# Last output projection of a two-layer trunk: the order of one product, when its weight sums are added, and how many planner steps the side work takes

## The chip, the cores and the metric

The kernel runs on one core of a Trainium2 chip. The metric is the device time of one execution in microseconds (us). The engines are named as in the profile: PE does the matrix products (PEld its weight loads), DVE, ACT and POOL are the vector, scalar and GpSimd engines, SP only issues DMAs. POOL issues DMAs as well, and all the accumulating ones.

## What is computed

Two layers over 256 tokens of width 2048. Each layer normalizes x, projects it, runs four branches (sparse attention, retention, a gated recurrence, cross-attention), gates and sums them, and adds an output projection:

```
merged = sum over n of sigmoid(gate_n) * (branch_n @ w_branch[n])
x = x + merged @ w_out
```

The change lies in the last of these, `merged @ w_out` of layer 1 and what comes after it: a product of 256 x 2048 by 2048 x 2048, added to x and stored.

## The kernel before

**Number format.** Each float32 factor is split into a rounded high part and a remainder (`whi`, `wlo` for weights; `...h`, `...l` for the other side), and three fast products replace one: high by high, low weight by high, high weight by low. Making the parts of a tile costs one ACT copy (`cut_piece`, line 433) and one DVE subtraction that waits for it (line 435).

**Units.** Weights come in slabs of 512 x 512, each used in two half slabs. A half slab of an ordinary slab (both token halves) is 12 matmuls, a half slab of a "product" (one token half) is 6. There are four buffers of weight parts: parts are cut four half slabs ahead of their use, and the ACT copy of a cut waits until PE has finished the half slab four before.

**The last stage.** The four output columns are numbered 0 to 3. Columns 0 and 1 are done plainly, in slabs (column, row block), for the merged blocks `mg0`, `mg3`, `mg2`, `mg1` in that order. Columns 2 and 3 together are done with one product in eight saved (a Strassen-Winograd scheme): seven products 0 to 6, whose left sides are sums of quarters of the merged matrix, called forms (product 1 uses form `s3`, 3 uses `s1`, 4 uses `s2`, 0 uses `r4`; 2, 5 and 6 use plain quarters), and whose right sides are weights or sums of weight blocks. The sums are built in memory by accumulating DMAs: chain `sumy` passes through products 2, 3, 4 and 6 (the next block is added behind each cut, `LAST_NEXT`), chain `sumx` serves product 1 alone: four base loads on SP, four accumulating DMAs on POOL. Products 0 and 5 use raw weights.

`LAST_ORDER` (line 160) is the order, written by hand: slabs as pairs, products as numbers. In this document half slabs of the stage are counted from 0. Before: (0,0) is 0 and 1, (1,0) 2 and 3, (0,1) 4 and 5, product 2 is 6 to 9, (1,1) 10 and 11, (0,2) 12 and 13, product 1 is 14 to 17, product 3 is 18 to 21, (1,2) 22 and 23, (0,3) 24 and 25, product 4 is 26 to 29, product 0 is 30 to 33, (1,3) 34 and 35, product 5 is 36 to 39, product 6 is 40 to 43. A number in `LAST_BEGIN` says how many half slabs ahead of its product's first one a DMA stage is issued, counted in cuts. Before, the `sumx` base loads come in front of cut 14 - 30 = -16, its adds in front of cut -6; the first `sumy` loads in front of cut -4.

**Side work and the planner.** Everything that isn't a slab is a task, a generator that is resumed between half slabs: `advance` (line 501) calls `Stream.pump` (210) and then cuts the next half slab. `pump` allows two steps behind a slab's half slab and one behind a product's, and none while the planner's account of DVE or ACT stands over `LATE` = 2500 ns behind its account of PE; a task is resumed only when PE's account has passed the end of its last step by `MARGIN` = 500 ns. The account's costs are in lines 111 to 142: a DVE operation of n elements per partition 155 + 1.05 n ns (1230 for 1024, 693 for 512), an ACT copy 215 + 0.8 n (1034 for 1024), a half slab 2720 on PE, one of a product 1360. When a product needs a form that isn't there, its task is forced on (`stream.until`, line 1591). The planner only fixes the order of the instructions in each engine's queue; the engines then run as their waits allow.

**The tasks of the stage.** `merged(d)` (1433) turns a merged block round: a DVE transpose (`mgpi`), 16 small DMAs (`mgp`), a rest of three or four ticks, then `split` (`mg...h` on ACT, `mg...l` on DVE). For block 1, the last, all 16 DMAs go through POOL; the others alternate between POOL and SP. `last_forms` (1442) makes the forms; each is two DVE operations over 512 (`total`, 1270, one planner step each) and two parts (`parts`, 1276, one step each). `second_column` (1556) recombines column 3 behind product 0: `qs - us`, then `us = qs + ...`, then a POOL DMA that adds the residual onto `us`, then `xc - qs`; `us` is stored by SP five ticks later. Product 6 needs `xc - qs` and forces the task on (1594). Behind products 5 and 6, `first_column` (1579) adds on DVE and stores a token half of column 2; the one behind product 6 is the end of the kernel's work.

```
ps, t = {0: (0, 1), 1: (0, 1), 2: (0, 0), 3: (1, 0), 4: (1, 1), 5: (0, 0), 6: (1, 0)}[i]
...
if i == 6 and "less" not in got:
    stream.until(got["second"], lambda: "less" in got)
```

Of the kernel before, what the change touches and what calls it, by code (L numbers as in the profile page):

```python
# [154 lines left out]
DUO, AHEAD, FIRST, MERGED = (2, 0, 3, 1), 10, 0, (0, 3, 2, 1)  # L155
# [1 line left out]
STAGES = ((False, 1, 1), (True, 0, 1), (False, 0, 0), (True, 0, 1), (True, 1, 1))  # L157
LAST_SUM, RING, EARLY = (True, 1, 0), 5, 8
BETWEEN_PRODUCTS = (4, 3, 4, 4, 3, 2, 3)
LAST_ORDER = ((0, 0), (1, 0), (0, 1), 2, (1, 1), (0, 2), 1, 3, (1, 2), (0, 3), 4, 0, (1, 3), 5, 6)  # L160
LAST_RAW, LAST_NEXT = {0: (1, 1), 5: (1, 0)}, {2: (True, 0, 1), 3: (True, 1, 1), 4: (True, 1, 0)}
LAST_BEGIN = {2: ((AHEAD, "y", (False, 0, 0)),), 1: ((3 * AHEAD, "x", (False, 0, 1)), (2 * AHEAD, "x", (True, 1, 1)))}
MOVES, STEPS, BANKS, WARM = 5, 2, 2, 7
MARGIN, LATE = 500.0, 2500.0

# [123 lines left out]
def gemm_plan(wmem, win, wbr, wout):  # L289
# [22 lines left out]
    def last_product(l, i, part):  # L312
# [3 lines left out]
        if not part:  # L316
            for ahead, chain, stage in LAST_BEGIN.get(i, ()):
                begins[len(cuts) - ahead] = chain, stage
# [5 lines left out]
    for l in range(L):  # L324
# [18 lines left out]
        if l + 1 < L:  # L343
# [3 lines left out]
            continue  # L347
        for at in LAST_ORDER:
            if isinstance(at, tuple):
# [14 lines left out]
def trunk(ctx: ExitStack, tc: tile.TileContext, x, xt, memt, ng, qkg, hg, lbl, win, wmem, wbr, wout,  # L364
# [16 lines left out]
    def G(shape, name, dt=F32):  # L381
        return gen.tile(shape, dt, tag="g", name=name)
# [169 lines left out]
    def blocks(u):  # L552
        return u.rearrange("p h (b c) -> p h b c", c=32)
# [670 lines left out]
    for l in range(L):  # L1224
# [45 lines left out]
        def total(out, sign, first, second):  # L1270
            for p in range(2):
                at, a, b = (u[p] if isinstance(u, tuple) else blocks(u[:, 4 * p:4 * p + 4, :]) for u in (out, first, second))
                (ve.tensor_add if sign > 0 else ve.tensor_sub)(at, a, b)
                yield

        def parts(name, out):
            hi, lo = (spool.tile([128, 8, 128], F32R, tag="s", name=name + e) for e in "hl")
            ac.copy(hi, out)
            yield
            ve.tensor_sub(lo, out, hi.bitcast(F32))  # L1280
            yield
            return hi, lo
# [25 lines left out]
        def sigmoid(gt, t, src):  # L1308
            ac.activation(gt[:, t, :], src, AF.Sigmoid, scale=rs[:, t:t + 1])
# [35 lines left out]
        def both(us):  # L1345
            for t in range(2):
                sigmoid(us, t, us[:, t, :])
                yield
            return us
# [92 lines left out]
        def last_forms():  # L1442
            def quarter(b, t):
                return tuple(last_rows[b + p][:, :, 4 * t:4 * t + 4] for p in range(2))

            while not (0 in last_rows and 1 in last_rows):
                yield BLOCKED
            r4 = G([128, 8, 128], "r4")
            yield from total(r4, -1, quarter(0, 0), quarter(0, 1))
            last_made["s3"] = yield from parts("s3", r4)  # L1450
            while len(last_rows) < 4:
                yield BLOCKED
            s1, s2 = (G([128, 8, 128], name) for name in ("s1", "s2"))
            yield from total(s1, -1, quarter(0, 1), quarter(2, 1))
            last_made["s1"] = yield from parts("s1", s1)
            yield from total(s2, -1, s1, quarter(0, 0))
            last_made["s2"] = yield from parts("s2", s2)
            yield from total(r4, 1, s2, quarter(2, 0))
            last_made["r4"] = yield from parts("r4", r4)

        def gated(pg):
# [76 lines left out]
        xh, rs = nx, stream.add(scale_of(nssq, list(nx), 1))  # L1538

    last_ready = stream.add(last_forms())  # L1540
    open_chunks, ends, got = {}, {}, {}

# [13 lines left out]
    def second_column():  # L1556
        qs, us = got["qs"], got["us"]
        ve.tensor_tensor(qs, qs, us[:, 0:1, :].to_broadcast([128, 2, 512]), op=OP.subtract)
        yield
        ve.tensor_tensor(us, qs, us[:, 1:2, :].to_broadcast([128, 2, 512]), op=OP.add)  # L1560
        po.dma_start(us, x1[:, :, 3 * 512:4 * 512], accum_op=OP.add)
        yield
        ve.tensor_sub(got["xc"][:, 1, :], got["xc"][:, 1, :], qs[:, 1, :])
        got["less"] = True
        yield from stream.rest(5)
        sy.dma_start(out[:, :, 3 * 512:4 * 512], us)
# [17 lines left out]
    def last_take(i, part):  # L1584
# [15 lines left out]
        if i == 2:  # L1600
            got["us"] = G([128, 2, 512], "us")
            ac.copy(got["us"][:, 0, :], to)
        elif i == 1:
            got["qs"] = G([128, 2, 512], "qs")
            ac.activation(got["qs"][:, 1, :], to, AF.Copy, scale=-1.0)
        elif i == 3:
            ac.copy(got["us"][:, 1, :], to)
            got["xc"] = residual(2)
        elif i == 4:
            ve.tensor_add(got["us"][:, 0, :], got["us"][:, 0, :], to)  # L1610
        elif i == 0:
            ac.copy(got["qs"][:, 0, :], to)
            got["second"] = stream.add(second_column())
        else:
            first_column(i - 5, to)

    for at in LAST_ORDER:
        if isinstance(at, tuple):
# [61 lines left out]
```

## Time and profile before

| | us |
|---|---|
| median of 3 runs (1820.14 to 1822.33) | 1821.0 |
| the profiled execution | 1821.62 |
| its span in the trace | 1819.9 |
| PE busy | 1799.6 |
| DVE busy | 1369.0 |
| ACT busy | 1077.7 |
| POOL busy | 400.7 |

A trace row gives the start, the duration, the engine, the line, the operation and its tiles (output <- inputs), and in brackets how long the engine had stood idle and what ended that. All helper calls show line 127 (DVE, ACT, POOL) or 145 (PE), so rows are told apart by tiles: `wo` is a plain slab's result, `px` a product's. A PE row's duration is longer than its share, because matmuls overlap: the distance between starts is what counts. "SPq" rows are DMA issues on SP. The DMA list gives, for each kind of issue, the queue, the count, KB of one and the median us from issue to landing.

### The profile page before, as it was taken

What the parts mean: (1) busy time and instruction counts of PE and PEld (TensorE: products, weight loads), DVE (VectorE), ACT (ScalarE), POOL (GpSimd) and SP (SyncE); (2) the same over time, 40 slices, a digit from 0 to 9 for tenths busy, and PEclk for the clock granted to TensorE, in tenths of its full rate; (3) what the DMA queues carried; (4) which work ended last, traced back from release to release, by engine and by line L of the source; (5) the groups of instructions that cost most, each with busy time, mean ns of one, the idle gap of its engine ahead of it and who ended that gap; (6) DMA issues with size and microseconds to landing.
All of it is one profiled execution on the core that took longest, in us unless ns stands there. A gap on an engine that the chain in (4) does not pass through costs nothing.

```text
span 1819.9 us, 24386 instructions
## 1 busy us (share of the span) xinstructions
PE 1799.6 (99%) x8812; PEld 1495.5 (82%) x8812; DVE 1369.0 (75%) x1482; ACT 1077.7 (59%) x1283; POOL 400.7 (22%) x599
## 2 busy tenths in 40 slices
PE   9999999999999999999999999999999999999996
PEld 7889888888888888888888888888888888888875
DVE  5677798786878777677666788887787967767785
ACT  4756565456667656564465656545566755656363
POOL 0022320033332111102123241003322211010420
PEclk9999999999999999999999999999999999999998
DMA  9769965789999899977785995668999989998996
GB/s 330 270 213 288 289 206 187 252 231 268 286 256 285 271 232 273 262 228 243 237 276 173 325 260 180 226 235 243 251 273 279 290 246 240 285 251 274 267 245 182
DMA packets 127401, 459.84 MB, mean 253 GB/s; under 512 B 23472, under 2 KB 44720, under 8 KB 95024
## 3 DMA queue, kind: packets, MB, share of 16 engines
q1 hardware_dynamic: 89200, 356.14, 55.9%
q0 software_dynamic: 37792, 101.88, 28.9%
q8 instruction: 69, 1.13, 0.2%
q14 instruction: 52, 0.43, 0.1%
q10 hardware_dynamic: 288, 0.26, 0.0%
HBM read 428.05 MB, written 6.29 MB: 239 GB/s over the span
## 4 chain that ended last, share of the span: by engine, by line
PE 91%; DMA 4%; DVE 2%; issue 1%; ACT 1%; POOL 0%; SPq 0%; ACTq 0%; DVEq 0%; POOLq 0%
PE u L145 49%; PE px L145 21%; PE bw L145 9%; PE wo L145 5%; PE mv L145 2%; PE mk L145 2%; DMA sumy<-in_wout 1%; DMA mgp<-mgpi 1%; DVE wlo L127 1%; DMA raw<-in_wbr 1%; PE ixrp L145 0%; ACT whi L127 0%; PE mov L145 0%; PE mlg L145 0%; PE bo L145 0%
## 5 line engine op out<-in xcount | busy, mean ns | idle before, releaser
L127 DVE TENSOR_TENSOR wlo<-raw,whi 128x1024 fp32r<-128x1024 f32 (+3 forms) x548 | 644.7, 1186 | 315.7 <-ACT whi L127 309.5
L127 ACT CAST whi<-raw 128x1024 fp32r<-128x1024 f32 (+3 forms) x548 | 559.4, 1024 | 542.9 <-PE u L145 343.3
L127 DVE TENSOR_TENSOR wlo<-sum,whi 128x1024 fp32r<-128x1024 f32 x240 | 288.1, 1220 | 62.6 <-ACT whi L127 55.9
L127 ACT CAST whi<-sum 128x1024 fp32r<-128x1024 f32 x240 | 250.5, 1052 | 99.1 <-PE px L145 51.3
L127 POOL DMA_DIRECT2D sum<-in_win x152 | 137.2, 909 | 608.3 <-DVE wlo L127 560.1
L127 POOL DMA_DIRECT2D mgp<-mgpi x72 | 40.1, 610 | 133.9 <-DVE mgpi L127 67.5
L145 PE MATMUL u<-whi,x01h 128*128 128x512 f32 (+2 forms) x176 | 67.5, 384 | 0.0
L145 PE MATMUL u<-whi,x11h 128*128 128x512 f32 (+2 forms) x176 | 67.5, 384 | 0.0
L145 PE MATMUL u<-whi,x12h 128*128 128x512 f32 (+2 forms) x176 | 67.5, 383 | 0.0
L145 PE MATMUL u<-whi,x02h 128*128 128x512 f32 (+2 forms) x176 | 67.5, 383 | 0.0
L145 PE MATMUL u<-whi,x10h 128*128 128x512 f32 (+2 forms) x176 | 67.4, 383 | 0.0
L145 PE MATMUL u<-whi,x00h 128*128 128x512 f32 (+2 forms) x176 | 67.4, 383 | 0.0
L145 PE MATMUL u<-whi,x13h 128*128 128x512 f32 (+2 forms) x176 | 67.2, 382 | 0.0
L145 PE MATMUL u<-whi,x03h 128*128 128x512 f32 (+2 forms) x176 | 67.2, 382 | 0.0
L145 PE MATMUL u<-wlo,x13h 128*128 128x512 f32 (+2 forms) x176 | 67.1, 381 | 0.0
L145 PE MATMUL u<-wlo,x11h 128*128 128x512 f32 (+2 forms) x176 | 67.1, 381 | 0.0
L145 PE MATMUL u<-wlo,x01h 128*128 128x512 f32 (+2 forms) x176 | 67.1, 381 | 0.0
L145 PE MATMUL u<-wlo,x02h 128*128 128x512 f32 (+2 forms) x176 | 67.1, 381 | 0.0
L145 PE MATMUL u<-wlo,x12h 128*128 128x512 f32 (+2 forms) x176 | 67.1, 381 | 0.0
L145 PE MATMUL u<-wlo,x00h 128*128 128x512 f32 (+2 forms) x176 | 67.1, 381 | 0.0
L145 PE MATMUL u<-wlo,x10h 128*128 128x512 f32 (+2 forms) x176 | 67.1, 381 | 0.0
L145 PE MATMUL u<-whi,x10l 128*128 128x512 f32 (+2 forms) x176 | 67.1, 381 | 0.0
(536 smaller groups left out, 4590.8 us busy)
## 6 DMA issues: line engine op xcount, KB each, us to landing
raw<-in_win SPq DMA_DIRECT2D x180, 1024.0 KB, 6.4
sum<-in_win POOLq DMA_DIRECT2D x152, 512.0 KB, 8.5
sum<-in_win SPq DMA_DIRECT2D x80, 512.0 KB, 6.9
raw<-in_wbr SPq DMA_DIRECT2D x32, 1024.0 KB, 6.6
raw<-in_wout SPq DMA_DIRECT2D x28, 1024.0 KB, 6.7
raw<-in_wmem SPq DMA_DIRECT2D x12, 1024.0 KB, 6.7
sumy<-in_wout POOLq DMA_DIRECT2D x12, 512.0 KB, 10.4
raw<-in_win SPq DMA_DIRECT2D x8, 656.0 KB, 4.2
```

Source lines behind the costliest of these rows:

```text
L127: return call(*args, **kw)
L145: return self.engine.matmul(out, w, x, **kw)
```

## The change

- **Order.** Slab (1,2) moves ahead of products 1 and 3, and these two change places. New half slab numbers: (1,2) is 14 and 15, product 3 is 16 to 19, product 1 is 20 to 23; all others keep theirs. Product 1 is "the single product": it alone uses `sumx`.
- **`sumx`.** Its base loads are issued 34 half slabs ahead of product 1 (in front of cut 20 - 34 = -14), its accumulating DMAs 6 ahead (in front of cut 14).
- **Forms.** Both DVE operations of a form are done in one planner step; since nothing is yielded behind them, the ACT copy of the form's high part falls into the same step. A form takes two steps instead of four.
- **Recombination.** `second_column` does all its DVE operations and the POOL DMA in one step, the first one behind half slab 34 (the first of slab (1,3)).

```diff
-LAST_ORDER = ((0, 0), (1, 0), (0, 1), 2, (1, 1), (0, 2), 1, 3, (1, 2), (0, 3), 4, 0, (1, 3), 5, 6)
+LAST_ORDER = ((0, 0), (1, 0), (0, 1), 2, (1, 1), (0, 2), (1, 2), 3, 1, (0, 3), 4, 0, (1, 3), 5, 6)
...
-LAST_BEGIN = {2: ((AHEAD, "y", (False, 0, 0)),), 1: ((3 * AHEAD, "x", (False, 0, 1)), (2 * AHEAD, "x", (True, 1, 1)))}
+LAST_BEGIN = {2: ((AHEAD, "y", (False, 0, 0)),), 1: ((34, "x", (False, 0, 1)), (6, "x", (True, 1, 1)))}
...
+            def both(*at):
+                for _ in total(*at):
+                    pass
+
             while not (0 in last_rows and 1 in last_rows):
                 yield BLOCKED
             r4 = G([128, 8, 128], "r4")
-            yield from total(r4, -1, quarter(0, 0), quarter(0, 1))
+            both(r4, -1, quarter(0, 0), quarter(0, 1))
...
-            yield from total(s1, -1, quarter(0, 1), quarter(2, 1))
+            both(s1, -1, quarter(0, 1), quarter(2, 1))
             last_made["s1"] = yield from parts("s1", s1)
-            yield from total(s2, -1, s1, quarter(0, 0))
+            both(s2, -1, s1, quarter(0, 0))
             last_made["s2"] = yield from parts("s2", s2)
-            yield from total(r4, 1, s2, quarter(2, 0))
+            both(r4, 1, s2, quarter(2, 0))
...
         ve.tensor_tensor(qs, qs, us[:, 0:1, :].to_broadcast([128, 2, 512]), op=OP.subtract)
-        yield
         ve.tensor_tensor(us, qs, us[:, 1:2, :].to_broadcast([128, 2, 512]), op=OP.add)
         po.dma_start(us, x1[:, :, 3 * 512:4 * 512], accum_op=OP.add)
-        yield
         ve.tensor_sub(got["xc"][:, 1, :], got["xc"][:, 1, :], qs[:, 1, :])
```

## The prediction

> **What bounds the kernel now.** The page first: PE is the bound, and what can be won lies where PE stands still or ends early.
>
> ```profile
> PE 1799.6 (99%) x8812; PEld 1495.5 (82%) x8812; DVE 1369.0 (75%) x1482; ACT 1077.7 (59%) x1283; POOL 400.7 (22%) x599
> ```
>
> Second, one piece of the chain of waits gives the price of a slab, 24 matmuls in 5.44 us; a half slab is 2.72 and one of a product 1.36. Third, PE's rows in order of time through the last stage, which begins at 1718.08:
>
> ```profile
> 1685.61 5.44 PE bw L145 x24
> ```
>
> ```profile
> 1728.74 0.39 PE L145 MATMUL wo<-whi,mg0l 128*128 128x512 f32 x1
> 1730.90 0.50 PE L145 MATMUL wo<-whi,mg3h 128*128 128x512 f32 x1 [1.78 <-ACT mg3h L127]
> ...
> 1732.16 0.50 PE L145 MATMUL wo<-whi,mg3l 128*128 128x512 f32 x1 [0.53 <-DVE mg3l L127]
> ...
> 1737.28 0.39 PE L145 MATMUL px<-whi,mg0h 128*128 128x512 f32 x1
> ...
> 1775.46 0.39 PE L145 MATMUL px<-whi,s2h 128*128 128x512 f32 x1
> ...
> 1780.73 0.39 PE L145 MATMUL px<-whi,s2l 128*128 128x512 f32 x1
> 1783.20 0.50 PE L145 MATMUL px<-whi,r4h 128*128 128x512 f32 x1 [2.08 <-ACT r4h L127]
> ...
> 1786.12 0.80 PE L145 MATMUL px<-whi,r4l 128*128 128x512 f32 x1 [2.19 <-DVE r4l L127]
> ...
> 1787.14 0.63 PE L145 MATMUL px<-wlo,r4h 128*128 128x512 f32 x1
> ...
> 1789.27 0.45 PE L145 MATMUL px<-whi,r4h 128*128 128x512 f32 x1
> ...
> 1792.79 0.39 PE L145 MATMUL wo<-whi,mg1h 128*128 128x512 f32 x1
> ...
> 1808.89 0.39 PE L145 MATMUL px<-whi,mg1l 128*128 128x512 f32 x1
> ```
>
> ```profile
> 1785.00:1790.00 5.00, 3.88 (x10) 3.11 (x11) 1.71 (x2) 1.04 (x1) 0.00 (x0) 0.66 1.06 250
> ```
>
> Three losses stand there. (a) Slab (0,1) takes from 1728.97 to 1737.28, 8.3 us for 5.44: 2.9 lost waiting for `mg3`. (b) Product 0 takes from 1780.96 to 1792.79, 11.8 us against product 4's 5.5: 6.3 lost, 4.6 of it waiting for form `r4`, the rest because from 1786.12 to 1789.27 matmuls start 0.43 us apart and not 0.23, at a granted clock of 0.66 in that window. (c) PE ends at 1809.28, the span at 1819.9.
>
> Fourth, what ends that tail:
>
> ```profile
> 1795.21 1.22 DVE L127 TENSOR_TENSOR qs<-qs,us 128x1024 f32<-128x1024 f32 x1
> ...
> 1807.01 1.22 DVE L127 TENSOR_TENSOR us<-qs,us 128x1024 f32<-128x1024 f32 x1
> ...
> 1809.32 0.69 DVE L127 TENSOR_TENSOR xc<-px,xc 128x512 f32<-128x512 f32 x1 [0.49 <-PE px L145]
> ```
>
> ```profile
> 1808.53 1.09 POOL L127 DMA_DIRECT2D us<-x  x1 [27.65 <-DVE us L127]
> ```
>
> ```profile
> 1815.42 0.60 SPq L1566 DMA_DIRECT2D out<-us  x1
> ```
>
> ```profile
> out<-xc SPq DMA_DIRECT2D x4, 256.0 KB, 2.1
> xc<-x POOLq DMA_DIRECT2D x1, 512.0 KB, 16.8
> us<-x POOLq DMA_DIRECT2D x1, 512.0 KB, 6.9
> out<-us SPq DMA_DIRECT2D x1, 512.0 KB, 3.1
> ```
>
> The second operation of the recombination, `us`, runs 11.8 us behind the first. Its residual DMA then lands 6.9 later and its store is the last: 1815.42 + 3.1 = 1818.5, and 1.4 more to the end of the span.
>
> **The change part by part.** *Recombination in one step.* The planner put `us` behind product 5 because its account was over 2500 ns late there. Now it stands behind half slab 34. Product 0 ends 16.3 us before PE does (three units); `us` is done 4.8 us behind it (copy of `qs`, the cut in front, two operations of 1.2), POOL issues at 5.2, the DMA lands at 5.2 + 6.9 = 12.1. So it is hidden by 4 us of PE work, and `first_column`'s store is last: 1809.28 + 0.03 + 0.69 for `xc`, 2.1 to landing, 1.4 to the end, 1813.5 in the trace's own time. Gain 6.4. DVE's two further operations there, 1.8 us, stand before the cut for half slab 38, which has over 2 us to spare. Bound: at the 16.8 us of the other residual DMA `us` lands at 22, its store ends 6.5 us later than this.
>
> *Forms in two steps.*
>
> ```profile
> 1780.24 0.69 DVE L127 TENSOR_TENSOR r<-s,mgp 128x512 f32<-128x512 f32 x1
> 1780.85 3.49 DVE L127 TENSOR_TENSOR wlo<-raw,whi 128x1024 fp32r<-128x1024 f32 x3
> ...
> 1784.85 1.22 DVE L127 TENSOR_TENSOR r4l<-r,r4h 128x1024 fp32r<-128x1024 f32 x1
> ```
>
> ```profile
> 1729.81 1.04 ACT L127 CAST mg3h<-mgp 128x1024 fp32r<-128x1024 f32 x1 [3.83 <-DMA mgp<-mgpi]
> ...
> 1735.62 1.05 ACT L127 CAST s3h<-r 128x1024 fp32r<-128x1024 f32 x1 [1.91 <-DVE r L127]
> ...
> 1778.01 2.96 ACT L127 CAST whi<-raw 128x1024 fp32r<-128x1024 f32 x3
> 1781.16 1.04 ACT L127 CAST whi<-raw 128x1024 fp32r<-128x1024 f32 x1 [0.18 <-PE px L145]
> 1782.11 1.04 ACT L127 CAST r4h<-r 128x1024 fp32r<-128x1024 f32 x1
> ```
>
> Both parts of `r4` were forced in front of product 0, so they stood behind the cut for half slab 33, which waits for PE itself. Following the planner's rule with its own costs, the new steps come behind these half slabs (h and l: the high and low part): `s1` 10 (sums and h) and 12 (l), `s2` 13 and 14, `r4` 15 and 17. Before they were 10, 12, 13, 15; 18, 22, 23, 24; 25, 27 and forced. `r4` is thus complete some 15 us before product 0: loss (b) goes, gain 6.3.
>
> What is late next: I laid these orders out with the rows' durations: DVE one per 1.14 us (3.49 for three), ACT one per 0.95 (2.96 for three), a high part no sooner than the DVE sums it reads, as in the 1.91 us wait of `s3h`. The same working on the old order gives 2.7 us of waiting at half slab 4 and 4.9 at 30, where the rows show 2.8 and 4.6. In the new order three waits appear:
>
> - *Half slab 11.* With the `s3` steps earlier, the planner's account behind half slab 7 is 2134 ns late and not 2779, so the split of `mg1` goes there too, ahead of the cut for 11, three half slabs sooner.
>
> ```profile
> 1735.87 1.48 POOL L127 DMA_DIRECT2D mgp<-mgpi  x2
> ```
>
> ```profile
> mgp<-mgpi POOLq DMA_DIRECT2D x1, 32.0 KB, 7.2
> sumy<-in_wout POOLq DMA_DIRECT2D x1, 512.0 KB, 13.6
> ```
>
>   The last two DMAs of block 1 stand on POOL behind the first `sumy` add. That add I place at 1732.3, so they land about 1733 + 7.2 = 1740.3 to 1740.5; ACT, at `mg1h` from 1738, holds the cut behind it, whose DVE half ends 1.2 us too late. Bounds 0 (landing at 1738.7) and +2.7 (1742).
> - *Half slabs 18 and 19.* Each form's h is queued on ACT ahead of a cut and waits for DVE, which is then late for the next form. `r4h` holds the copy for 19, which ends about 1763.6, its DVE half 1.3 later; PE is ready for 19 at 1761.6. Wait 0.6 + 3.1. Bounds 0 (the planner's own account shows no delay) and 3.7 + 1.6.
> - *Half slab 21*: 0.7 behind `r4l`, bounds 0 and 0.7.
>
> *`sumx` adds moved.*
>
> ```profile
> 1689.06 3.66 POOL L127 DMA_DIRECT2D sumx<-in_wout  x4
> ...
> 1709.19 4.23 POOL L127 DMA_DIRECT2D mgp<-mgpi  x8 [2.18 <-DMA sumx<-in_wout]
> ```
>
> ```profile
> q0 software_dynamic: 298, 1.06, 58.6%
> q1 hardware_dynamic: 190, 1.43, 37.8%
> ```
>
> ```profile
> DMA to landing us min/median/max: 7.2/9.1/18.2
> ```
>
> These four held POOL's `mgp` DMAs until 1709.19, and POOL's queue took 58.6% of the DMA engines between 1690 and 1700 for 1.06 MB; the raw loads and SP's `mgp` DMAs ran beside them. `mg3h` waited 3.83 us for its DMAs until 1729.81. Twice 58.6% of 10 us, about 11.7 us of all DMA engines (an estimate, four adds being 2.1 MB), leaves this stretch; `mg3` must be some 3.4 us earlier to free PE. So loss (a) goes: gain 2.9, bounds 0 and 2.9; I take 2.9. The adds now follow the four `sumy` adds on POOL, about 1738 to 1742. At the longest landing, 18.2, the last is there at 1760, and the copy for half slab 23 wants it at about 1768: nothing. Behind them stand product 4's sums: the last is issued once half slab 19 is cut, about 1765.6, lands by 13.6 at 1779.2, wanted at 1778.4. Bounds 0 and +5.4 (at 18.2); I take 0, by the many shorter landings. The base loads on SP, two cuts later, move 2 MB by 5 us, long before the adds need them: nothing.
>
> *Order.* Slab (1,2) frees its raw buffer 8 cuts sooner, so raw loads and a residual load come earlier on SP; PE's work is the same. Zero. `s3` and `s1` are done before either product.
>
> **Sum.** Against the profiled 1821.62: -6.4 -6.3 -2.9 +1.2 +3.7 +0.7 = -10.0, so 1811.6. The median of the runs, 1821.0, is 0.6 lower: 1811.0.
>
> **The rivals.**
> - *No new waits*: the engines keep to the planner's account. 1821.0 - 15.6 = 1805.4. For it, bounds of 0 above; against it, the wait of `s3h`. 0.15.
> - *`mg3` still late*: SP's queue, not the adds, held it. 1811.0 + 2.9 = 1813.9. 0.12.
> - *The clock falls again* at half slabs 18 and 19. In the rows, waits of 4.6 us in all with two matmuls between brought matmuls at 0.43 us, those of 1.78 and 0.53 did not; 3.7 lies between. Eight matmuls at +0.2: 1812.6. 0.12. [...]
> - *The `us` store still ends last*, its DMA taking 16.8: 1811.0 + 6.5 = 1817.5. Against it, DMA traffic is lower by then (6.9 for the same DMA at the end). 0.07.
> - *The `r4` wait stays*, the step not taken where I say because the planner's clock runs otherwise: 1811.0 + 6.3 = 1817.3. 0.04.
> - *Slower*: the sums bind. `sumy`, `sumx`, `sumy` go through POOL's queue in a row, four adds each, from 1732.3. At 20 us for each four, product 4's last sum lands at 1792.3, half slab 29 starts at 1794.6, PE ends 1.4 + 5.5 + 16.3 later and a clock loss of 1.6 on top at 1819.4; with 4.2 of tail the span is 1823.6, the median 1824.7. It decides from about 20 us; the four `sumx` adds took from 1689.06 to about 1709, in the densest stretch of the trace, the `sumy` adds less. 0.04.
>
> **How the numbers follow.** The forecast has 0.46. The range runs from the case without new waits, with a little of the bounds, to `mg3` late and sums late together: 1805.5 to 1817.0. Faster by over 0.2% (3.6 us, about what a measurement of this kernel can tell from no change) is all but the last case and half of the two before it: 0.90; same 0.06; slower 0.04.
>
> **What the changed profile would show.** `us<-qs,us` on DVE near 1793 and the last store an `out<-xc`, 4 us behind PE's end (right), or `out<-us` last (wrong). No PE wait on `r4h` or `r4l`, granted clock 1.00 throughout. No wait on `mg3`; if one stands, the adds weren't the cause. PE waits with `whi` or `wlo` named in product 3, `r4h` just ahead on ACT. If `whi<-sumx` or `whi<-sumy` waits for a DMA while PE stands, the sums were moved too late, and the forecast fails by that wait.

## The result, and the profile after

The kernel after takes 1811.9 us (median of 5 runs, 1811.54 to 1812.43), the kernel before 1821.0 (median of the 5 runs beside them, 1819.33 to 1822.61): a ratio of 0.995, with a 95% interval from 0.9935 to 0.9964. The profiled execution of after took 1812.43 us, its span 1810.7. The forecast was 1811.0 with a range from 1805.5 to 1817.0.

The page's first part shows nothing of it. The matmuls are the same, and PE is as busy with them, in the last stage for 84.62 us before and for 84.28 now:

```profile
PE 1799.3 (99%) x8812; PEld 1495.8 (83%) x8812; DVE 1368.5 (76%) x1482; ACT 1076.7 (59%) x1283; POOL 400.6 (22%) x599
```

The view that shows it is PE's waits, cut to the last stage: engine and line, what was waited for, us in total, times, longest. First before, then after.

```profile
PE px L145 <- DVE r4l L127: 2.2, 1, 2.2
PE px L145 <- ACT r4h L127: 2.1, 1, 2.1
PE wo L145 <- ACT mg3h L127: 1.8, 1, 1.8
PE wo L145 <- DVE mg3l L127: 0.5, 1, 0.5
```

```profile
PE px L145 <- ACT whi L127: 2.7, 2, 1.8
PE px L145 <- DVE wlo L127: 2.4, 5, 0.8
PE wo L145 <- DVE wlo L127: 0.9, 1, 0.9
```

All four waits for forms and for `mg3` are gone, and 6.0 us of waits for cut weights have come in place of 6.6. What PE won is little: its last stage took 91.2 us before (1718.08 to 1809.28) and takes 90.4 now (1716.15 to 1806.55). PE's rows in order of time show where the new waits stand:

```profile
1727.03 0.39 PE L145 MATMUL wo<-whi,mg3h 128*128 128x512 f32 x1
...
1732.47 0.39 PE L145 MATMUL px<-whi,mg0h 128*128 128x512 f32 x1
...
1741.97 0.50 PE L145 MATMUL wo<-wlo,mg3h 128*128 128x512 f32 x1 [0.93 <-DVE wlo L127]
...
1758.90 0.50 PE L145 MATMUL px<-wlo,s1h 128*128 128x512 f32 x1 [0.28 <-DVE wlo L127]
1762.13 0.51 PE L145 MATMUL px<-whi,s1h 128*128 128x512 f32 x1 [1.81 <-ACT whi L127]
1763.39 0.50 PE L145 MATMUL px<-wlo,s1h 128*128 128x512 f32 x1 [0.75 <-DVE wlo L127]
...
1766.80 0.50 PE L145 MATMUL px<-wlo,s3h 128*128 128x512 f32 x1 [0.38 <-DVE wlo L127]
...
1781.50 0.51 PE L145 MATMUL px<-whi,s2h 128*128 128x512 f32 x1 [0.94 <-ACT whi L127]
1782.76 0.50 PE L145 MATMUL px<-wlo,s2h 128*128 128x512 f32 x1 [0.75 <-DVE wlo L127]
1784.02 0.40 PE L145 MATMUL px<-whi,r4h 128*128 128x512 f32 x1
1784.68 0.50 PE L145 MATMUL px<-wlo,r4h 128*128 128x512 f32 x1 [0.27 <-DVE wlo L127]
...
1790.06 0.39 PE L145 MATMUL wo<-whi,mg1h 128*128 128x512 f32 x1
```

Slab (0,1) takes 5.44 us, with no wait. Half slab 11 waits (1741.97), then product 3 at 18 and 19, product 1 at 21, product 4 twice at 29, product 0 at its second matmul. ACT's rows name the reasons, in the order of the terms: a split ahead of a copy that waits for its DMAs, a form's high part ahead of a copy that waits for DVE, and a copy that waits for a sum's DMA.

```profile
1738.47 1.05 ACT L127 CAST mg1h<-mgp 128x1024 fp32r<-128x1024 f32 x1 [2.44 <-DMA mgp<-mgpi]
...
1760.09 1.05 ACT L127 CAST r4h<-r 128x1024 fp32r<-128x1024 f32 x1 [3.82 <-DVE r L127]
...
1780.40 1.04 ACT L127 CAST whi<-sumy 128x1024 fp32r<-128x1024 f32 x1 [3.96 <-DMA sumy<-in_wout]
```

At the end, `us` is done at 1795.6, and the last store is one of `xc`:

```profile
1794.34 1.23 DVE L127 TENSOR_TENSOR us<-qs,us 128x1024 f32<-128x1024 f32 x1
```

```profile
1805.18 0.60 SPq L1568 DMA_DIRECT2D out<-us  x1
1807.31 0.33 SPq L1584 DMA_DIRECT2D out<-xc  x1
```

The span ends 4.15 us behind PE, where it was 10.6.

### The profile page after: what moved, and what is told of

It reads as the page before. It is cut to its first block, busy times and chain, and to the rows that moved or that the text cites. A ratio compares the mean times of both kernels' runs of the same rounds, so it can differ in the third digit from the quotient of the medians.

```text
span 1810.7 us, 24389 instructions
## 1 busy us (share of the span) xinstructions
PE 1799.3 (99%) x8812; PEld 1495.8 (83%) x8812; DVE 1368.5 (76%) x1482; ACT 1076.7 (59%) x1283; POOL 400.6 (22%) x599
## 4 chain that ended last, share of the span: by engine, by line
PE 97%; DMA 2%; issue 1%; POOL 0%; DVE 0%; ACT 0%; ACTq 0%; POOLq 0%
PE u L145 51%; PE px L145 22%; PE bw L145 10%; PE wo L145 6%; PE mk L145 2%; PE mv L145 2%; DMA sumy<-in_wout 2%; PE ixrp L145 0%; PE mov L145 0%; PE mlg L145 0%; PE bo L145 0%; PE co L145 0%; PE aov L145 0%; PE cl L145 0%; PE bs L145 0%
## 5 line engine op out<-in xcount | busy, mean ns | idle before, releaser
L145 PE MATMUL u<-wlo,x03h 128*128 128x512 f32 (+2 forms) x176 | 67.1, 381 | 0.0
L145 PE MATMUL u<-whi,x00l 128*128 128x512 f32 (+2 forms) x176 | 67.1, 381 | 0.0
```

The source lines that it names most:

```text
L145: return self.engine.matmul(out, w, x, **kw)
```

## The experiments

**Theory.** Three of the four edits take a wait away (`mg3`, `r4`, the late store), and two of them put other waits in its place: a form's high part in one step with its sums stands on ACT in front of a copy, and the `sumx` adds stand in POOL's queue in front of product 4's sums. **Rivals.** The end of the span became short by lighter DMA traffic and not by the step; `mg3` was held by SP's queue and not by the adds; product 4's sums are late because the copies in front of them are late.

The table holds all kernels that follow. Median and ratio to the kernel before (95% interval) are of all runs (before itself was measured again beside each of the three sets of experiments: 1821.1, 1820.4 and 1820.2); the other columns are of one profiled execution. A loss is the time from a step's first matmul to the next step's, less 5.44 us (so a wait for a step's very first matmul stands in the step before it; slow matmuls are in it, which start 0.43 us apart and not 0.23, as behind `r4`'s wait in before). "mg3" is slabs (1,0) and (0,1), "tail" the end of the span less PE's end.

| kernel | median us | ratio | stage starts | mg3 | half 11 | P3 | P1 | P4, P0 | P5, P6 | tail |
|---|---|---|---|---|---|---|---|---|---|---|
| before | 1821.0 | | 1718.1 | 2.9 | 0 | 0.1 | 0.1 | 6.4 | 0.2 | 10.6 |
| after | 1811.9 | 0.9935 to 0.9964 | 1716.2 | 0 | 1.3 | 3.7 | 0.7 | 2.9 | 0.2 | 4.2 |
| before, recombination in one step | 1815.0 | 0.9954 to 0.9979 | 1715.7 | 2.0 | 0 | 0.1 | 0.1 | 6.2 | 0.2 | 4.8 |
| before, forms in two steps | 1820.1 | 0.9988 to 1.0006 | 1716.8 | 4.4 | 1.1 | 0.6 | 3.4 | 0.1 | 4.1 | 5.6 |
| before, new order | 1820.5 | 0.9992 to 1.0010 | 1716.7 | 2.4 | 0 | 0.1 | 0.1 | 6.0 | 0.2 | 10.3 |
| before, `sumx` 8 cuts sooner | 1817.0 | 0.9975 to 0.9993 | 1715.9 | 0 | 0 | 0.1 | 0.1 | 7.2 | 0.2 | 10.3 |
| after, `sumx` as before | 1815.0 | 0.9955 to 0.9979 | 1715.8 | 4.3 | 1.3 | 4.7 | 1.9 | 0.1 | 0.2 | 4.2 |
| after, forms in four steps | 1819.2 | 0.9984 to 1.0002 | 1716.5 | 0 | 0 | 0.1 | 4.2 | 9.6 | 0.2 | 4.8 |
| after, high part with low | 1813.8 | 0.9949 to 0.9974 | 1716.9 | 0 | 0.9 | 0.1 | 3.1 | 5.1 | 0.2 | 4.1 |
| after, `sumx` at cuts -24, -14 | 1811.3 | 0.9939 to 0.9964 | 1716.2 | 0 | 6.2 | 1.5 | 0.7 | 0.1 | 0.2 | 4.1 |
| the same, forms in four steps | 1810.9 | 0.9934 to 0.9961 | 1715.6 | 0 | 0 | 0.1 | 0.1 | 7.0 | 0.2 | 4.8 |
| high with low, `sumx` at -24, -14 | 1805.6 | 0.9906 to 0.9933 | 1716.2 | 0 | 1.4 | 0.1 | 0.1 | 0.1 | 0.2 | 4.1 |
| the same, old order | 1810.5 | 0.9937 to 0.9962 | 1716.2 | 0 | 1.4 | 0.1 | 0.1 | 0.1 | 5.3 | 4.1 |
| the same, new order, `mg1` later | 1804.5 | 0.9900 to 0.9927 | 1716.8 | 0 | 0 | 0.1 | 0.1 | 0.1 | 0.2 | 4.1 |

### Each edit alone, on the kernel before

**The recombination in one step.** The two `yield` lines between its operations go, nothing else.

```
-        yield
         ve.tensor_tensor(us, qs, us[:, 1:2, :].to_broadcast([128, 2, 512]), op=OP.add)
         po.dma_start(us, x1[:, :, 3 * 512:4 * 512], accum_op=OP.add)
-        yield
```

> The kernel before with the recombination in one step and nothing else. Theory: the end of the span hangs on that step alone; the matmuls keep their waits for mg3 (2.3) and r4 (4.3 and the slow matmuls), PE ends about 1809 in the trace's time, the end of the span stands 4.2 us behind it and not 10.6, the last store is out<-xc: 1821.0 - 6.4 = 1814.6 us. Rival: the gain at the end came from the other edits (lighter DMA traffic made the residual's DMA fast), then the store of us still ends last and the time is within 2 us of 1821.0.

1815.0 us, 6.1 less, and the tail is 4.8, which is 5.8 less. In the profiled run (at 1812.35 the fastest of the five) `us` starts 12.8 us before PE ends (1792.95, PE's end 1805.76). The step gives the gain at the end without the other edits; the first rival falls.

**The forms in two steps.**

```
-yield from total(r4, -1, quarter(0, 0), quarter(0, 1))
+both(r4, -1, quarter(0, 0), quarter(0, 1))      # and so for s1, s2 and r4
```

> The kernel before with the forms' sums in one step with the high part, nothing else: old order of slabs, sumx adds where they were, recombination in three steps. By the planner's rule the steps come behind half slabs 10 and 12 (s1), 13 and 15 (s2), 20 and 23 (r4), and the recombination behind 34, 35 and 37, so that product 6 no longer waits for its last step. Theory: the wait for r4 goes (-6.3), the tail goes too (-6.4), the wait for mg3 stays, and new waits of about 0.4 to 0.9 at half slabs 6, 8, 11 and 19 and 2.4 at 17 come (+5.0): 1821.0 - 12.7 + 5.0 = 1813.3 us. Rival: no new waits without the other edits, 1808.3 us. Second rival: the tail stays, as the recombination is still in three steps, 1819.7 us.

1820.1 us: nothing to be measured, where 1813.3 was expected. The wait for `r4` is gone (product 0 takes 5.49), the wait in product 1 came as expected, but three things had been left out. The matmuls behind the waits for `mg3` and in product 1 ran slowly (1.6 us at each place, with seven starts in a row 0.43 us apart; more on this at the end); the tail is 5.6, not 4.2 (even so 5.0 us of it went without the recombination's edit, because the planner now issues `us` 10.6 us ahead of PE's end: that gain, too, is not one edit's alone); and products 5 and 6 lost 4.1 on a wait that the one for `r4` had covered, the raw load of product 5's slab. SP issues it at 1786.34, ACT waits for it until 1799.28:

```profile
1786.34 0.33 SPq L420 DMA_DIRECT2D raw<-in_wout  x1
```

```profile
1799.28 2.00 ACT L127 CAST whi<-raw 128x1024 fp32r<-128x1024 f32 x2 [5.80 <-DMA raw<-in_wout]
```

**The order alone**, the `sumx` cuts as they were:

```
-LAST_ORDER = (..., (1, 1), (0, 2), 1, 3, (1, 2), (0, 3), ...)
+LAST_ORDER = (..., (1, 1), (0, 2), (1, 2), 3, 1, (0, 3), ...)
-1: ((3 * AHEAD, ...), (2 * AHEAD, ...))
+1: ((36, ...), (26, ...))
```

> The kernel before with the new order of the last stage alone: slab (1,2) ahead of products 3 and 1, sumx loads and adds at the cuts where they stood before, forms in four steps and recombination in three. Theory: the order moves no PE work; mg3's wait, r4's wait with its slow matmuls and the late last store all stay: 1821.0 us within 1.5. What it does is to free a raw buffer sooner, so that product 5's slab is loaded earlier, which nothing waits for while r4's wait covers it. Rival: the order itself gives part of the gain: 1818 us or less.

1820.5, no change, as both the prediction and this expectation have it.

**The `sumx` loads and adds alone**, but sooner and not later than before, since in the old order they can't go later:

```
-1: ((3 * AHEAD, "x", ...), (2 * AHEAD, "x", ...))
+1: ((38, "x", ...), (28, "x", ...))
```

> The kernel before with nothing changed but the sumx loads and adds, 8 cuts sooner (cuts -24 and -14 of the last stage). Theory: the adds alone held the mgp DMAs, so the wait for mg3 goes and the waits for r4 and the late last store stay: 1821.0 - 2.9 = 1818.1 us. Rival: SP's queue and not the adds held mg3: 1821.0 us with the wait for mg3 still there.

1817.0. The wait for `mg3` is gone and the rest stays: the adds held it, and the second rival falls. (The base loads moved as well, but sooner here and later in after, and the wait goes in both.) In before, POOL stood still in front of its `mgp` DMAs until `sumx` adds had landed, in four waits of 12.7 us together:

```profile
POOL mgp L127 <- DMA sumx<-in_wout: 12.7, 4, 4.6
```

The view of DMAs over 1680 to 1715 (last number: median us to landing) shows the rest, first before, then this kernel. POOL issued 17 of its `mgp` DMAs in that time and not 24, and those of SP took 12.7 us to land and not 5.6:

```profile
mgp<-mgpi POOLq DMA_DIRECT2D x17, 32.0 KB, 5.8
mgp<-mgpi SPq DMA_DIRECT2D x10, 32.0 KB, 12.7
```

```profile
mgp<-mgpi POOLq DMA_DIRECT2D x24, 32.0 KB, 5.4
mgp<-mgpi SPq DMA_DIRECT2D x19, 32.0 KB, 5.6
```

Against the runs of before beside each, the edits alone gave 6.1 us (one step), 3.2 (adds sooner) and, with an interval that holds no change, 0.9 (forms) and -0.1 (order).

### One edit taken back, on the kernel after

**The `sumx` loads and adds where they were.**

```
-1: ((34, "x", (False, 0, 1)), (6, "x", (True, 1, 1)))
+1: ((36, "x", (False, 0, 1)), (26, "x", (True, 1, 1)))
```

> The kernel after with the sumx loads and adds back at the cuts where they stood before (adds ahead of the mgp DMAs of the last stage), all else as after. Theory: the sumx adds in POOL's queue caused both, the wait for mg3 before and product 4's late sums after; mg3's wait returns (+2.9) and the waits at half slabs 28, 29 and 30 go (-2.8): 1811.9 + 0.1 = 1812.0 us. Rival: the late sums come from the late copy for half slab 19 (r4h queued in front of it) and the residual loads on SP; then they stay late: 1811.9 + 2.9 = 1814.8 us. Second rival: mg3's wait had another cause and doesn't return: 1809 to 1812 us with no PE wait on mg3.

1815.0. The number is the rival's, the mechanism is the theory's: product 4 and product 0 lose nothing (5.49 each), though `r4h` still holds the copy for half slab 19. The last sum is issued at 1767.64 and lands 6.5 us later, where after's took 16.7, and its copy waits for PE alone:

```profile
1782.67 1.05 ACT L127 CAST whi<-sumy 128x1024 fp32r<-128x1024 f32 x1 [1.66 <-PE wo L145]
```

So the late sums came from the adds ahead of them, and the late copy doesn't suffice. The wait for `mg3` returned. That it costs 3.1 us and not 0.1 is by slow matmuls: `mg3` costs 4.3 and not 2.9, and the two long waits in product 3, the same as after's to 0.01, are followed by matmuls 0.43 us apart into product 1.

**The forms in four steps.**

```
-both(r4, -1, quarter(0, 0), quarter(0, 1))      # and so for s1, s2 and r4
+yield from total(r4, -1, quarter(0, 0), quarter(0, 1))
```

> The kernel after with the forms in four steps each as before, all else as after. By the planner's rule r4's high part comes behind half slab 28 and its low part is forced in front of product 0. Theory: the waits at half slabs 11, 18, 19 and 21 go (-5.65), since no high part stands in front of a copy any more; the wait for r4 returns, 4.3 and 1.6 of slow matmuls (+5.9); and the copy for half slab 19 being on time, the last sum of product 4 is issued 3 us or more sooner and its waits go too (-2.8): 1811.9 - 2.6 = 1809.3 us, so that the forms in one step cost more than they give. Rival: product 4's sums are late by the sumx adds ahead of them in POOL's queue whatever the copy does: 1812.1 us, with whi<-sumy still waiting for a DMA by 4 us at half slab 29.

1819.2, 10 us above what was expected and 7 above the rival's number, though the rival's mechanism is there (`whi<-sumy` for half slab 29 waits 2.98 us for its DMA). No form's high part delays product 3 any more, so product 1 starts 4.5 us sooner (1760.11, after: 1764.64), and now its own sums are late. ACT waits for three of the four:

```profile
1759.42 1.05 ACT L127 CAST whi<-sumx 128x1024 fp32r<-128x1024 f32 x1 [2.19 <-DMA sumx<-in_wout]
1762.80 1.05 ACT L127 CAST whi<-sumx 128x1024 fp32r<-128x1024 f32 x1 [2.33 <-DMA sumx<-in_wout]
...
1766.14 1.05 ACT L127 CAST whi<-sumx 128x1024 fp32r<-128x1024 f32 x1 [1.35 <-DMA sumx<-in_wout]
```

Product 4's sums are late again as well, though the last is issued 6.2 us sooner (1757.46, after: 1763.63); it takes 21.5 us to land, which ends the third rival; and then `r4` is late, with slow matmuls behind it (the mean granted clock of this profiled run is 0.998, of after's 1.000). In the kernel after, the waits of product 3 cover what the moved adds cost product 1.

### Toward a kernel without these waits

**The high part with the low, not with the sums.** One step holds the sums, the next the high and the low part, so that ACT finds the sums made.

```
 def both(*at):
     for _ in total(*at):
         pass
+    yield
 ...
-yield from parts(...)     # h, yield, l, yield
+yield from pair(...)      # h, l, yield
```

> The kernel after with each form in two other steps: the sums alone, then the high and the low part together, so that the high part never stands on ACT in front of a copy while its sums are still queued on DVE. By the planner's rule r4's parts come behind half slab 17. Theory: the waits at half slabs 18, 19 and 21 go (-4.4), since they came from the high part's place; but product 1's copies then meet the sumx adds, the last of which lands at about 1765.9, as where the forms took four steps (waits of 4.2 us in product 1, 2.2 in product 4): 1811.9 - 4.4 + 3.5 = 1811.0 us. Rival: the sums are in time, 1807.5 us. Second rival: the waits of product 3 stay, so the place of the high part wasn't their cause: 1811.9 us with product 3 still at 9.2 us.

1813.8. The waits in product 3 and the one at half slab 21 are gone: the place of the high part was their cause. And again product 1 (3.1) and products 4 and 0 (5.1, of which 1.6 are slow matmuls; mean granted clock 0.999) wait for their sums instead: product 4's last one takes 21.9 us to land. So by the medians the mended step is slower than the flawed one by 1.9 us, though one of its five runs, 1811.51, was as fast as after's.

**The `sumx` adds sooner, not later**: loads at cut -24, adds at -14, a stretch in which after's POOL issues nothing (1642 to 1686).

```
-1: ((34, "x", (False, 0, 1)), (6, "x", (True, 1, 1)))
+1: ((44, "x", (False, 0, 1)), (34, "x", (True, 1, 1)))
```

> The kernel after with the sumx loads at cut -24 and the adds at cut -14 of the last stage (8 cuts ahead of where they stood before, 28 ahead of after), where POOL issues nothing for 44 us; all else as after. Theory: the adds are then neither in front of the mgp DMAs nor of product 4's sums: mg3's wait stays away, product 4's waits (2.25) and the one at half slab 30 (0.55) go, the waits at 11, 18, 19 and 21 stay: 1811.9 - 2.8 = 1809.1 us. Rival: the DMA traffic is only moved into a stretch where it delays weight loads or the mgp DMAs as before: 1812 us or more.

1811.3. `mg3` is in time and products 4 and 0 lose nothing, as expected: the last sum lands 6.4 us behind its issue at 1766.45, and its copy at 1779.30 waits for PE alone. The late copy for half slab 19 is in this kernel as it is in after, so this settles that the adds made those sums late. But half slab 11 and the matmuls behind it lost 6.2 and not 1.3 (mean granted clock 0.998, after: 1.000): `mg1h` waits 4.70 us for its DMAs here, 2.44 in after, because POOL stood still on an earlier small DMA in the middle of that block's 16:

```profile
1730.69 2.64 POOL L127 DMA_DIRECT2D mgp<-mgpi  x5 [3.79 <-DMA mgp<-mgpi]
```

SP's issues, too, run 1.3 to 3.3 us later from 1700 on than in the kernel with both mended (below), whose stage starts at the same time. Why this is so, when that kernel and the next have the same adds, stays open. All five runs took over 1810.5 us, so it seems not to be a matter of the profiled one alone; the 0.6 us by which the median lies below after's is within the spread of either.

**The same adds, with the forms in four steps** (the diff of the adds, and that of the four steps above).

> The kernel after with the forms in four steps as before and the sumx loads and adds at cuts -24 and -14. Theory: with the adds out of the way the waits of products 1 and 4 for their sums go, and none of the waits from a high part ahead of a copy is there; only r4's wait and its slow matmuls are left (4.3 to 4.9 and 1.6): 1805.6 - 1.4 + 6.2 = 1810.4 us, no slower than forms in two steps with the same adds (1811.3), so that the forms' step as after made it gives nothing by itself. Rival: the waits of products 1 and 4 had another cause and stay: 1815 us or more.

1810.9, as expected, and the only loss is `r4`'s: 7.0, of which 2.8 are slow matmuls (mean granted clock 0.998). So beside the early adds the forms as after made them (1811.3) gave nothing. Without the unexplained part of that kernel's wait at half slab 11, about 5 us by its trace, they might have: no run shows it.

**Both mended** (the diff of `both` and `pair`, and that of the adds).

> The kernel after with both: forms as sums, then high and low part together, and the sumx loads and adds at cuts -24 and -14. Theory: of the waits in the last stage only the one at half slab 11 (1.25) stays: 1811.9 - 3.7 - 0.7 - 2.8 = 1804.7 us. Rival: a further wait takes their place, product 5's raw load or the sumy adds, each landing 10 to 14 us behind its issue: 1807 to 1809 us, with that wait in PE's rows.

1805.6. The two edits gave -1.9 (the wrong way) and 0.6 us alone, and 6.3 together; against the runs of before beside each, -2.5, 0.0 and 5.7. Only half slab 11 still waits, and it costs 1.4: the 6.2 that it cost with the adds alone didn't come back.

**With the old order.**

```
-LAST_ORDER = (..., (1, 1), (0, 2), (1, 2), 3, 1, (0, 3), ...)
+LAST_ORDER = (..., (1, 1), (0, 2), 1, 3, (1, 2), (0, 3), ...)
-1: ((44, ...), (34, ...))
+1: ((38, ...), (28, ...))
```

> The best version so far with the old order of the last stage (products 1 and 3 ahead of slab (1,2)), the sumx adds at the same cuts of the stage, all else the same. Theory: the order alone was worth nothing beside r4's wait, but with that wait gone it decides when a raw buffer is free for product 5's slab: as in the kernel with the forms alone, that load is issued about 11 us ahead of product 5 and lands 13 us later, and products 5 and 6 wait 3 to 4 us: 1805.6 + 3.9 = 1809.5 us. Rival: the raw load is in time without the late sums' traffic beside it: 1805.6 us.

1810.5: the order, worth nothing beside `r4`'s wait, is worth 4.9 us without it. Product 5's raw load is issued at 1777.64 and lands 14.7 us later, ACT waits 7.65 us for it, and of the 5.3 us that products 5 and 6 lose some 1.6 are slow matmuls behind that wait (mean granted clock 0.999):

```profile
1792.42 1.99 ACT L127 CAST whi<-raw 128x1024 fp32r<-128x1024 f32 x2 [7.65 <-DMA raw<-in_wout]
```

**With `mg1` split later**, for the last wait:

```
-(3, (po,) if l + 1 == L else (po, sy))
+((5, (po,)) if l + 1 == L else (3, (po, sy)))
```

> The best version so far (forms as sums, then high and low part; sumx adds at cut -14) with the step that splits mg1 two ticks later, so that it comes behind half slab 10 and not behind 7, no longer ahead of the copies for half slabs 11 to 13. Theory: the wait at half slab 11 is the split of mg1 waiting on ACT for its last two DMAs; it goes, and no wait is left in the last stage: 1805.6 - 1.4 = 1804.2 us. Rival: the later split delays the s1 sums and product 3 waits for form s1 instead: 1805.6 us or more.

1804.5, the lowest of all, 0.990 to 0.993 of the kernel before. PE's waits in the last stage are an empty list, and from 1717 to 1799 it is busy for 81.78 of 82 us at the full clock (the eighth column of the second line is the granted clock):

```profile
core 0: us, PE busy (x) PEld busy (x) DVE busy (x) ACT busy (x) POOL busy (x), PEclk, DMA share, GB/s
1717.00:1799.00 82.00, 81.78 (x360) 67.22 (x358) 70.24 (x67) 52.04 (x54) 21.34 (x30) 1.00 0.89 234
```

## Why the prediction was right, point by point

- **The tail**, -6.4: right. 6.45 in the two traces; with the recombination alone 5.8 in the trace and 6.1 in the median.
- **`mg3`**, -2.9: right in size and cause, shown by the adds moved alone and by the adds put back.
- **`r4`**, -6.3: the wait is gone, its slow matmuls too; the granted clock is 1.00 in every stretch of 5 us of the stage.
- **The three new waits**, +1.2, +3.7, +0.7: measured 1.25, 3.7 and 0.7, at the places named, with `mg1h` and `r4h` ahead on ACT. The kernel with the high part elsewhere shows the cause of the second and third, the one with the later split that of the first.
- **Product 4's sums**, taken as 0 with an upper bound of 5.4: this term was mis-sized. It is 2.25 in product 4, and 0.55 in product 0 behind it. The last sum is issued at 1763.63 and used at 1780.40, 16.8 us later, and needed 16.7 to land. "By the many shorter landings" chose the wrong rows: the view with 7.2, 9.1 and 18.2 us is of all eight `sumx` DMAs of before, four of them plain loads on SP (median 8.4); the four adds alone have a median of 14.1, and no row of before has adds with four others ahead. The adds moved late were the cause, as the rival on the slower side had it, but with 2.8 us and not enough to decide. A wait of `whi<-sumy` for a DMA while PE stands is the sign that the prediction itself had named for sums moved too late.
- **The `sumx` adds at their new place**, taken as "nothing" with the last there at 1760 at the longest landing, 18.2: they took 22.5 us (median), and the copy at 1765.92 still waited 0.99 us for the last. PE lost nothing by it only because the waits of product 3 had made product 1 late. Where those waits are gone, product 1 loses 3.1 to 4.2.
- **What made up for it.** By the terms the trace should be 7.2 us shorter than before's (0.8 in the stage, 6.45 behind it); it is 9.2. The rest is that the last stage starts at 1716.15 and not 1718.08. What the change moves ahead of the stage isn't the reason: three kernels that share before's code up to the stage start it at 1715.7, 1716.8 and 1716.7. By the traces, before's profiled execution was 0.8 us behind after's when POOL issued its first `mk0pt` DMA (95.9 us), and fell back another 1.15 between 1315 and 1384, long before anything that the change touches; why, no experiment looked into. So the total came out within 0.9 us partly by two errors of 2.8 and 1.9 us with opposite signs.
- **The order**, 0: right alone. But without it most of `r4`'s 6.3 is lost again, as the forms without the new order (products 5 and 6 lose 4.1) and the best kernel with the old order (5.3) show. The prediction named the raw loads that the order brings forward, and put them at zero: it didn't ask what waits for them once `r4` is on time.
- **The clock**, a rival at 0.12: it didn't fall at half slabs 18 and 19 in after (1.00 from 1763 to 1768); in the kernel with the adds put back it did (0.50 from 1767 to 1772), behind the same waits. So the prediction's reading, by which the length of the waits decides, isn't borne out, and that it didn't fall in after was in part luck.

What the sum hid is that its terms don't add. Late adds cost 2.8 us of waits beside those of product 3, and 8.2 without them (1813.8 against 1805.6 with the mended step); and the forms are worth 7.4 us beside the late adds (1819.2 against 1811.9) and nothing beside the early ones (1810.9 against 1811.3, which has the unexplained wait at half slab 11 in it).

## What to carry to other kernels

A wait that goes uncovers the next one, so ask of each edit what is late once the others are in, and price a moved DMA by everything that is queued behind it at its new place. If two edits that ought to help hinder each other, mend both before either is judged: here each mend alone gave 0.6 us or less (one of the two with a wait of unexplained size in it), both together 6.3. Put an instruction that must wait for another engine's fresh result a step behind it, not in the same step, when something urgent is queued behind: here product 3 lost 3.7 us with the high part in the step of its sums, and 0.1 with it in the next.

## What the runs showed of the hardware

**Adds behind other adds in POOL's queue landed later: 15.4 and 20.0 us against 9.9.** The same `sumy` adds of 512 KB, from 1735 to 1765, with the median us to landing last: the best kernel but one (adds early), after, and after with forms in four steps.

```profile
sumy<-in_wout POOLq DMA_DIRECT2D x7, 512.0 KB, 9.9
```

```profile
sumy<-in_wout POOLq DMA_DIRECT2D x7, 512.0 KB, 15.4
sumx<-in_wout POOLq DMA_DIRECT2D x4, 512.0 KB, 22.5
```

```profile
sumy<-in_wout POOLq DMA_DIRECT2D x7, 512.0 KB, 20.0
sumx<-in_wout POOLq DMA_DIRECT2D x4, 512.0 KB, 23.3
```

The `sumx` adds themselves, issued at cut -14 with no `sumy` add ahead, landed in 14.4 us (median of the four) in the kernel with both mended and in 14.3 in before with them sooner, and in 22.5 and 23.3 behind four `sumy` adds.

**The same waits slow the matmuls in one run and not in another.** In product 3, PE waited 1.81 and 0.76 us in the kernel with the adds put back and 1.81 and 0.75 in after. There the granted clock fell to 0.50, here it stayed at 1.00 (windows of 5 us right behind the waits, put back first):

```profile
1767.00:1772.00 5.00, 4.60 (x11) 3.64 (x12) 5.00 (x6) 3.46 (x5) 0.86 (x1) 0.50 1.00 173
```

```profile
1763.00:1768.00 5.00, 4.22 (x17) 3.19 (x18) 5.00 (x6) 4.01 (x6) 0.86 (x1) 1.00 1.07 248
```

There is a second such pair at `mg3`. Behind waits of 1.78 and 0.53 us in before the granted clock stayed at 1.00 (1729 to 1734) and the matmuls from 1732.50 on started 0.23 us apart; behind waits of 1.70 and 0.52 in before with the forms alone they started 0.43 us apart from 1731.37 to 1733.93. Behind `r4`'s wait in before the granted clock was 0.50 for 3.41 us (1786.0 to 1789.4), with starts 0.43 us apart from 1786.71 to 1789.27; in the kernel with the adds put back it was 0.50 throughout the window above and 0.65 from 1770 to 1775. What makes the clock fall in one run and not in the other, no experiment tested.
